# Modulation rows of a diffusion trunk: multiply-adds on VectorE and one sum over partitions in place of TensorE products

## The chip, the cores and the metric

The kernel runs on one core of a Trainium2 chip. A core has five engines with instruction queues of their own: TensorE (PE; its weight loads are listed apart as PEld), VectorE (DVE), ScalarE (ACT), GpSimd (POOL) and SyncE (SP), which here only issues DMAs. TensorE writes to PSUM, which has eight banks of 512 fp32 columns over 128 partitions; the other operands lie in SBUF. The metric is the device time of one execution in microseconds. The kernel before took 1547.54, 1547.64 and 1549.52 us in three runs, 1547.64 in the median.

## The reference

One inference step of two interleaved layers, in fp32, with width 1024, for 512 latent tokens and 128 context tokens. Layer 0 mixes by neighbourhood attention over a grid of 8 by 64 (NA), layer 1 by grouped-query attention with rotary positions (GQA). A gated feed-forward net with a convolution of width three (FFN) follows each. Around every sub-layer stand RMS norms, and a shift, a scale and a gate that come from a condition vector:

```python
def adaln(cond, w, b):
    m = jax.nn.silu(cond) @ w + b
    return jnp.split(m[..., None, :], 6, axis=-1)
...
    sh_ap, sc_ap, g_ap, sh_fp, sc_fp, g_fp = adaln(c_ctx, ada_w[l], ada_b[l])
    sh_as, sc_as, g_as, sh_fs, sc_fs, g_fs = adaln(c, ada_w[l], ada_b[l])
    hp = rmsnorm(xp, norm_mix_pre[l]) * (1.0 + sc_ap) + sh_ap
    ...
    xs = xs + g_as * rmsnorm(os_.reshape(bs, ts, -1) @ w_o, norm_mix_post[l])
    hs = rmsnorm(xs, norm_ffn_pre[l]) * (1.0 + sc_fs) + sh_fs
```

There are two condition vectors (latents, context), so one modulation row of a layer is a product of a 2x1024 matrix with 1024x1024 weights, plus a bias, times a norm's gain where there is one. Each layer has six such rows.

## The kernel before

The program runs through the stages input norm, NA, its output projection, FFN 0, GQA, its projection, FFN 1. Products with weights are made of three fp32r products of high and low parts: ScalarE rounds a weight tile to its high part `wh`, VectorE or GpSimd subtracts for the low part `wl` (`wsplit`, L174 to L180), TensorE multiplies.

The NA stage runs over 16 heads. For each head (class `Head`), TensorE forms the scores `s` of four slots, VectorE adds the bias table and finds the extremum in one operation on PSUM (L964), ScalarE takes the exponential `p` with its sum (L968), VectorE takes the reciprocal `rc` (L971), GpSimd scales `p` with it (L972), TensorE turns `p` into `tp` (L120), VectorE or ScalarE copies it out as `pk` (L985, L987), and TensorE multiplies with the values (`po`). GpSimd also builds the next head's bias table `tb` from a mask and shifted runs (L927, with two SBUF inputs) and the low parts `wl` (L180, the same). Into the steps of a head the program puts pieces of the projections to q, k and v, a `stream` of parts: one `fill` is one part, six products for q or k. VectorE helps to take q and k out of PSUM (`qs` at L878, `kl` at L850).

The order of TensorE's work is that of the program text: `mm` and `turn` chain each instruction to the one before. In the NA stage a written list per head sets it, `ORDER0`, `ORDER`, `ORDER2`: `f` is a fill, `s0` to `s3` the scores of the next head, `t0` to `t2` the turns of this one, `v` the values, `p0` to `p2` steps of the context, `a` a step of the modulation rows. The order on the other engines and of the DMAs is set by a scheduler with its own model of durations. Every queue is worked off in order: an instruction that waits holds those behind it.

Three modulation rows of layer 0 are made in the NA stage: index 2 (gate of the mixer, times a gain), 4 (scale of the FFN, with 1 added and times a gain) and 3 (shift of the FFN). Generator `ada_work` does it: each step loads two blocks of 128 features by 1024 columns (`wr<-in_ada_w`, L293) and makes eight products with two blocks that were loaded a step before. The stationary operand is 32 columns of `scolp`, of which the first two hold the two conditions' features; the moving operand is the raw block, in four pieces of 256 columns that go to four groups of 32 output partitions of one PSUM bank, `ada`. The bank collects over eight blocks. Then VectorE adds the bias (L319) and applies the gain (L322), and two small DMAs store the row to `modrow`, from where it is broadcast in the next stages (L352). The same generator makes the other rows later in the program.

## Time and profile before

| What | Value |
|---|---|
| median of three runs | 1547.64 us (1547.54 to 1549.52) |
| span of the profiled execution, first to last instruction | 1546.0 us |
| what the median has beyond that span | 1.64 us |
| granted TensorE clock, mean | 0.999 |
| TensorE busy in the span | 1512.8 us (98%) |
| VectorE busy in the span | 1024.1 us (66%) |
| ScalarE, GpSimd busy | 854.2 us (55%), 701.8 us (45%) |
| first and last product of the three rows | 82.0 and 269.8 us |

The profile is one execution, instruction by instruction. A group's row gives line, engine, operation, output and inputs by the program's tile names, their shapes and the count; then the busy time and the mean of one in ns; then the engine's idle time just before them and what ended it. A row of the order of time gives start, length, engine, line and operation, with idle time before it in brackets. A row by stretch gives start and end, length, and for PE, PEld, DVE, ACT and POOL the busy time with the count in brackets, then the clock, the DMA engines' share and GB/s. An fp32 product stands in the trace as two records. Lines named L180 and the like are lines of the kernel before.

### The profile page before, as it was taken

Reading aid. Unit: us, or ns where it says so; the run is one execution under the profiler, and the core shown is the slowest. Engines: PE = TensorE matmul, PEld = TensorE weight load, DVE = VectorE, ACT = ScalarE, POOL = GpSimd, SP = SyncE. Lnnn points to the kernel's source line nnn. Section 1 sums busy time; section 2 is a strip of 40 time slices with the busy share of each in tenths; the row PEclk is TensorE's granted clock in tenths of the full one; section 3 lists DMA queues with packets and bytes.
Section 4 is the critical chain, followed back from the end, with each engine's and each line's share of the span. In section 5 each row is a group of like instructions: output and inputs, shape, how many; then the busy total and the mean of one; then the engine's idle time right before and its main releaser. Section 6 shows DMA issues by size and latency. Waiting matters only on the chain.

```text
span 1546.0 us, 26097 instructions
## 1 busy us (share of the span) xinstructions
PE 1512.8 (98%) x9709; PEld 1344.4 (87%) x9709; DVE 1024.1 (66%) x1648; ACT 854.2 (55%) x1624; POOL 701.8 (45%) x606
## 2 busy tenths in 40 slices
PE   6999999999999999999999999999999999999998
PEld 5988998888999999978887878878899999988886
DVE  4553453659877666756757877773988887786554
ACT  5665564646655555654544447763666655554443
POOL 1554463432355455525444464532235666542433
PEclk9999999999999999999999999999999999999999
DMA  9745454253565665388574421015433334447664
GB/s 318 210 122 159 122 132 116 64 190 124 183 224 177 221 190 162 114 277 272 178 234 155 129 69 42 2 40 190 153 114 115 119 111 156 132 164 252 226 221 131
DMA packets 196666, 243.99 MB, mean 158 GB/s; under 512 B 11484, under 2 KB 153020, under 8 KB 196540
## 3 DMA queue, kind: packets, MB, share of 16 engines
q1 hardware_dynamic: 186704, 235.74, 47.7%
q10 hardware_dynamic: 9836, 6.59, 2.5%
q8 instruction: 76, 1.25, 0.3%
q14 instruction: 50, 0.41, 0.1%
HBM read 214.38 MB, written 26.34 MB: 156 GB/s over the span
## 4 chain that ended last, share of the span: by engine, by line
PE 66%; DVE 5%; ACT 2%; issue 2%; POOL 1%; DMA 1%; POOLq 0%; DVEq 0%; ACTq 0%
PE acc L117 19%; PE ux L117 18%; PE uz L117 8%; PE gp L117 5%; PE uy L117 4%; PE po L117 3%; PE y L117 3%; PE s L117 2%; PE tp L120 2%; PE ada L117 1%; DMA wr<-in_ffn_w_up 1%; DVE t L1281 1%; ACT gp L1692 1%; PE tr L120 0%; DVE xo L400 0%
## 5 line engine op out<-in xcount | busy, mean ns | idle before, releaser
L180 POOL TENSOR_TENSOR wl<-wr,wh 128x1024 fp32r<-128x1024 f32 x70 | 173.3, 2480 | 238.5 <-ACT wh L178 223.5
L1204 POOL TENSOR_TENSOR wl<-wr,wh 128x1024 fp32r<-128x1024 f32 x76 | 183.5, 2435 | 46.9 <-ACT wh L1203 43.3
L117 PE MATMUL ux<-B,wh 128*128 128x322 f32 x832 | 200.1, 311 | 0.9 <-ACT u L1258 0.9
L1281 DVE SCALAR_TENSOR_TENSOR t<-C,cw,t 128x644 f32<-128x644 f32 x176 | 156.3, 888 | 51.3 <-ACT t L1279 50.7
L117 PE MATMUL acc<-wh,alo 128*128 128x512 f32 x440 | 172.3, 392 | 0.3 <-DVE alo L1173 0.3
L178 ACT CAST wh<-wr 128x1024 fp32r<-128x1024 f32 x140 | 145.6, 1048 | 48.5 <-DMA wr<-in_ffn_w_down 37.4
L117 PE MATMUL acc<-wh,ahi 128*128 128x512 f32 x440 | 171.9, 391 | 0.0
L117 PE MATMUL acc<-wl,ahi 128*128 128x512 f32 x440 | 171.8, 391 | 0.0
L117 PE MATMUL uz<-B,wh 128*128 128x322 f32 x640 | 156.2, 312 | 0.9 <-ACT v L1258 0.9
L117 PEld LDWEIGHTS ux<-B,wh 128*128 128x128 f32 x832 | 143.6, 189 | 3.4 <-issue 1.2
L1173 DVE TENSOR_TENSOR alo<-ain,ahi 128x384 fp32r<-128x384 f32 (+1 forms) x88 | 84.0, 973 | 84.9 <-ACT ahi L1171 84.0
L117 PE MATMUL ux<-B,wl 128*128 128x322 f32 x416 | 129.5, 311 | 2.7 <-DVE wl L1204 2.7
L117 PE MATMUL qk<-hT,wh 128*128 128x384 f32 (+1 forms) x512 | 122.4, 315 | 0.0
L117 PEld LDWEIGHTS uz<-B,wh 128*128 128x128 f32 x640 | 110.9, 189 | 4.3 <-ACT v L1258 1.5
L1204 POOL TENSOR_TENSOR vl<-wr,vh 128x1024 fp32r<-128x1024 f32 x38 | 96.3, 2535 | 24.6 <-ACT vh L1203 24.3
L1203 ACT CAST wh<-wr 128x1024 fp32r<-128x1024 f32 x84 | 84.8, 1049 | 40.8 <-DVE wr L1227 40.5
L1279 ACT ACTIVATE t<-C,cw 128x644 f32<-128x644 f32 x88 | 78.6, 893 | 47.8 <-DVE C L1309 40.3
L180 DVE TENSOR_TENSOR wl<-wr,wh 128x1024 fp32r<-128x1024 f32 x70 | 91.3, 1315 | 20.1 <-ACT wh L178 19.5
L117 PE MATMUL uz<-B,wl 128*128 128x322 f32 x320 | 99.6, 311 | 0.3 <-POOL wl L1204 0.3
L117 PEld LDWEIGHTS acc<-wh,alo 128*128 128x128 f32 x440 | 82.5, 188 | 18.8 <-DVE alo L1173 1.1
L117 PEld LDWEIGHTS acc<-wl,ahi 128*128 128x128 f32 x440 | 82.6, 188 | 17.9
L117 PEld LDWEIGHTS acc<-wh,ahi 128*128 128x128 f32 x440 | 82.6, 188 | 17.8
(259 smaller groups left out, 3857.7 us busy)
## 6 DMA issues: line engine op xcount, KB each, us to landing
wr<-in_ffn_w_up SPq DMA_DIRECT2D x88, 512.0 KB
wr<-in_ffn_w_down SPq DMA_DIRECT2D x88, 512.0 KB
wr<-in_ada_w SPq DMA_DIRECT2D x72, 512.0 KB
act<-act SPq DMA_DIRECT2D x44, 321.0 KB
wr<-in_na_w_qkv SPq DMA_DIRECT2D x24, 512.0 KB
mod<-modrow SPq DMA_DIRECT2D x20, 512.0 KB
ain<-act SPq DMA_DIRECT2D x44, 192.0 KB
wf<-in_ada_w SPq DMA_DIRECT2D x16, 512.0 KB
```

The costliest lines, as they stand in the source:

```text
L117: pe(nc.tensor.matmul(*a, **k))
L120: pe(nc.tensor.transpose(*a, **k))
L178: i = nc.scalar.copy(hi, raw)
L180: j = (low or nc.vector).tensor_sub(lo, raw, f32(hi))
L1173: pin(nc.vector.tensor_sub(lo[:, 0 : c1 - c0], ain[:, 0 : c1 - c0], f32(hi[:, 0 : c1 - c0])))
L1203: nc.scalar.copy(hl[0], src)
L1204: low.tensor_sub(hl[1], src, f32(hl[0]))
L1279: nc.scalar.activation(t, taps(0), AF.Identity, bias=cw[:, 3, n : n + 1], scale=cw[:, 1, n : n + 1])
L1281: nc.vector.scalar_tensor_tensor(t, taps(d), cw[:, w, n : n + 1], t, op0=ALU.mult, op1=ALU.add)
L1692: nc.scalar.activation(self.pt[i].rearrange("p (a b) -> p a b", a=2), sv, AF.Exp, bias=nm, scale=-1.0, accum_out=su)
```

## The change

For the three rows of the NA stage a new generator, `ada_vec`, takes the place of `ada_work`. It goes by half rows of 512 columns. A block is 128 features by 512 columns. For each of the two conditions VectorE multiplies the block by the condition's column of `scolp` (one number for each partition) and adds it to `acc`, the first block by a plain multiplication, the other seven by a multiply-add. After eight blocks `acc` holds 128 partial sums for each column, and TensorE adds them over the partitions: eight products with a stationary operand `one`, whose column q is one and the rest zero, moving 128 columns of `acc` at a time. VectorE adds the bias and applies the gain, now on 128x128, in place in `abias`, and the row's half is stored. The generator is advanced at every third fill after the first 20, and not by steps `a` of the written lists; `lag` leaves one more advance between the last multiply-add and the sum. `ada_work` itself stays for the other rows.

```diff
--- before.py
+++ after.py
@@ -39,7 +39,6 @@
 QW = T + 64
 NPT = 6
 NPK = 6
-NAR = 2
 OW = {0: 0, 2: 1, 4: 2}
 OEARLY = 2
 TH = 322
@@ -47,10 +46,10 @@
 NC = 3
 QKH = (slice(0, 256), slice(256, T))
 CTX = 2
-ORDER0 = "f f f t0 s0 f s1 t1 f f t2 f a f f s2 s3 f f f f f".split()
+ORDER0 = "f f f t0 s0 f s1 t1 f f t2 f f f s2 s3 f f f f f".split()
 ORDER = (
-    "f f t0 s0 f s1 t1 f f t2 f a f f s2 s3 f f f f f f".split(),
-    "p0 f f t0 s0 f s1 t1 f t2 p1 f f f v a p2 s2 s3 f f f".split(),
+    "f f t0 s0 f s1 t1 f f t2 f f f s2 s3 f f f f f f".split(),
+    "p0 f f t0 s0 f s1 t1 f t2 p1 f f f v p2 s2 s3 f f f".split(),
 )
 ORDER2 = (
     "t0 s0 s1 f f f t1 f f t2 f s2 f s3 f f f f f f f".split(),
@@ -328,6 +327,69 @@
                 for _ in range(n if steps == 1 else i < n):
                     load()
                 yield
+
+    def ada_vec(p, todo, lag=1):
+
+
+
+        one = p.tile([P, 2, 32], F32, name="one")
+        nc.gpsimd.memset(one, 0.0)
+        for q in range(2):
+            nc.gpsimd.memset(one[:, q, q : q + 1], 1.0)
+        bias = p.tile([P, P], F32, name="abias")
+        gr = p.tile([P, P], F32, name="again")
+        nc.gpsimd.memset(bias, 0.0)
+        nc.gpsimd.memset(gr, 0.0)
+
+        def pieces(row, half):
+            return row[512 * half : 512 * half + 512].rearrange("(j c) -> j c", j=4)
+
+        units = deque((l, idx, half, k) for l, idx in todo for half in range(2) for k in range(KC))
+        raws = deque()
+
+        def load():
+            if units:
+                l, idx, half, k = units.popleft()
+                c0 = idx * D + 512 * half
+                raw = p.tile([P, 512], F32, tag="wr", name="wr", bufs=3)
+                nc.sync.dma_start(raw, A["ada_w"][l, k * P : k * P + P, c0 : c0 + 512])
+                raws.append((l, idx, half, k, raw))
+
+        for _ in range(3):
+            load()
+        yield
+        while raws:
+            l, idx, half, k, raw = raws.popleft()
+            if k == 0:
+                acc = p.tile([P, 2, 512], F32, tag="acc", name="acc")
+                for q in range(2):
+                    nc.sync.dma_start(bias[q::32, :], pieces(A["ada_b"][l, idx * D : idx * D + D], half))
+                    if idx in gain_of:
+                        nc.sync.dma_start(gr[q::32, :], pieces(A[gain_of[idx]][l], half))
+            for q in range(2):
+                col = scolp[:, 2 * k + q : 2 * k + q + 1]
+                if k == 0:
+                    nc.vector.tensor_scalar(acc[:, q], raw, col, None, op0=ALU.mult)
+                else:
+                    nc.vector.scalar_tensor_tensor(acc[:, q], raw, col, acc[:, q], op0=ALU.mult, op1=ALU.add)
+            load()
+            if k < KC - 1:
+                yield
+                continue
+            for _ in range(lag):
+                yield
+            ps = bk.get("ada")
+            for q in range(2):
+                for j in range(4):
+                    mm(ps[32 * j : 32 * j + 32, 0:P], one[:, q], acc[:, q, j * P : j * P + P], start=q == 0, stop=q == 1)
+            nc.vector.tensor_add(bias, ps[:, 0:P], bias)
+            bk.put(ps)
+            if idx in gain_of:
+                nc.vector.scalar_tensor_tensor(
+                    bias, bias, 1.0 if idx in (1, 4) else 0.0, gr, op0=ALU.add, op1=ALU.mult
+                )
+            for q in range(2):
+                nc.scalar.dma_start(pieces(modrow[l][idx][q], half), bias[q::32, :])
 
     def drain(gen):
         for _ in gen:
@@ -1051,13 +1113,15 @@
 
         work = stream()
         l_ada = ExitStack()
-        ada0 = ada_work(
-            l_ada.enter_context(pool("ada")), l_ada.enter_context(pool("adar", NAR)), NAR, 1, ((0, 2), (0, 4), (0, 3))
-        )
+        ada0 = ada_vec(l_ada.enter_context(pool("ada")), ((0, 2), (0, 4), (0, 3)))
+        fills = [0]
 
         def fill(n=1):
             for _ in range(n):
                 next(work, None)
+                fills[0] += 1
+                if fills[0] > PRO and fills[0] % 3 == 0:
+                    next(ada0, None)
 
         fill(PRO)
         next(ada0)
@@ -1074,8 +1138,6 @@
                 if step == "f":
                     if i < len(order) - 1 or h % 4 or not h:
                         fill()
-                elif step == "a":
-                    next(ada0, None)
                 elif step[0] == "s" and nxt:
                     nxt.scores(int(step[1]))
                 elif step[0] == "t":
```

Where the instructions now stand on VectorE, at two places of the NA stage. The first is where the q and k of the first pair of heads are taken out of PSUM, up to the first scores (`kl`, `kh`: low and high part of k; `s,nm`: scores with their extremum). Before:

```order
L850 TENSOR_TENSOR kl_620<-tk,kh_754 64x128
L849 CAST kh_754<-qk 64x256
L850 TENSOR_TENSOR kl_620<-qk,kh_754 64x256
L849 CAST kh_753<-qk 64x384
L850 TENSOR_TENSOR kl_619<-qk,kh_753 64x384
L849 CAST kh_754<-qk 64x384
L850 TENSOR_TENSOR kl_620<-qk,kh_754 64x384
L964 ISA s,nm<-s,tb_615 128x384
```

With the change (L911 and L912 are the former L849 and L850, L1026 the former L964):

```order
L912 TENSOR_TENSOR kl_619<-qk,kh_750 64x256
L374 SCALAR_TENSOR_TENSOR acc<-wr,scolp,acc 128x512
L911 CAST kh_751<-qk 64x256
L912 TENSOR_TENSOR kl_620<-qk,kh_751 64x256
L374 SCALAR_TENSOR_TENSOR acc<-wr,scolp,acc 128x512 x2
L911 CAST kh_750<-qk 64x384
L912 TENSOR_TENSOR kl_619<-qk,kh_750 64x384
L374 SCALAR_TENSOR_TENSOR acc<-wr,scolp,acc 128x512
L911 CAST kh_751<-qk 64x384
L912 TENSOR_TENSOR kl_620<-qk,kh_751 64x384
L1026 ISA s,nm<-s,tb_615 128x384
```

Four multiply-adds of the first half row now stand among these steps, ahead of the first scores. The second place is some 80 us later, where the scores of slots 2 and 3 of a head are reduced and their reciprocals taken (`rc`). Before:

```order
L850 TENSOR_TENSOR kl_622<-qk,kh_1830 64x256
L964 ISA s,nm<-s,tb_616 128x384
L964 ISA nm 128x1
L964 ISA s,nm<-s,tb_616 128x384
L964 ISA nm 128x1
L850 TENSOR_TENSOR kl_621<-qk,kh_1829 64x384
L971 RECIPROCAL rc<-su 128x1
L850 TENSOR_TENSOR kl_622<-qk,kh_1830 64x384
L971 RECIPROCAL rc<-su 128x1
```

With the change:

```order
L374 SCALAR_TENSOR_TENSOR acc<-wr,scolp,acc 128x512 x3
L1026 ISA s,nm<-s,tb_616 128x384
L1026 ISA nm 128x1
L1026 ISA s,nm<-s,tb_616 128x384
L1026 ISA nm 128x1
L912 TENSOR_TENSOR kl_621<-qk,kh_1887 64x384
L374 SCALAR_TENSOR_TENSOR acc<-wr,scolp,acc 128x512
L1033 RECIPROCAL rc<-su 128x1
L374 SCALAR_TENSOR_TENSOR acc<-wr,scolp,acc 128x512
L912 TENSOR_TENSOR kl_622<-qk,kh_1888 64x384
L1033 RECIPROCAL rc<-su 128x1
```

Three multiply-adds now stand ahead of the reductions, and one ahead of each reciprocal.

## The prediction

> **What bounds the kernel now.** First the page: spans, busy shares and the chain that ended last.
>
> ```profile
> span 1546.0 us, 26097 instructions
> PE 1512.8 (98%) x9709; PEld 1344.4 (87%) x9709; DVE 1024.1 (66%) x1648; ACT 854.2 (55%) x1624; POOL 701.8 (45%) x606
> PE 66%; DVE 5%; ACT 2%; issue 2%; POOL 1%; DMA 1%; POOLq 0%; DVEq 0%; ACTq 0%
> ```
>
> Then the busy time by stretch: the NA stage from where the new VectorE work starts to where it ends, and what follows up to the FFN.
>
> ```profile
> 52.00:272.00 220.00, 218.67 (x1695) 199.24 (x1694) 95.90 (x284) 127.70 (x344) 119.19 (x121) 1.00 0.53 141
> 272.00:335.00 63.00, 61.39 (x344) 50.57 (x343) 32.57 (x74) 37.07 (x94) 23.31 (x30) 1.00 0.30 94
> ```
>
> The columns behind the length are PE, PEld, DVE, ACT and POOL busy. TensorE is busy for 218.67 of 220 us at full clock, so the stage lasts as long as its products, and it can gain from idle time at most 1.3 us. VectorE has 124 us free, on average. A microsecond of products taken out is a microsecond won, as long as nothing that TensorE waits for comes later.
>
> **Products removed and added.** Groups of the stage, by form:
>
> ```profile
> L117 PE MATMUL ada<-wr,scolp 128*32 128x256 f32 x192 | 12.8, 385 | 0.0
> L117 PE MATMUL po<-ptp,vt 128*64 128x128 f32 x32 | 2.6, 282 | 0.0
> ```
>
> The 96 products of the three rows (each is two records) cost 12.8 us, 0.067 us a record. They go. Instead come six blocks of eight products with 128 columns, 96 records in all. No row has 32x128 products of this kind. If their price goes by columns, a record costs half of 0.067, and the six blocks 3.2 us; if by record, 6.4 us. The other 128-column group has 0.081 us a record with half as many column groups side by side, which halved is 0.04. I take 0.0375, 0.6 us a block and 3.6 us in all. **TensorE: 12.8 - 3.6 = 9.2 us less** (6.4 to 9.6).
>
> **VectorE work added.** 84 multiply-adds and 12 multiplications on 128x512, six additions and four gain steps on 128x128. Nearest rows (min/median/max ns in the first, mean of one in the second):
>
> ```profile
> L419 DVE SCALAR_TENSOR_TENSOR xm<-xm,ro,mod x30: 737/746/2883, 339.4 to 1110.5; 128x512 f32<-128x512 f32 x30
> L597 DVE TENSOR_SCALAR xT<-xT,gcol,hcol 128x512 f32<-128x512 f32 x8 | 4.3, 543 | 2.1 <-ACT hT L596 2.0
> ```
>
> The first is the same operation on the same shape, with both inputs in SBUF. So 14 x 0.75 + 2 x 0.54 = 11.6 us for each half row, with some 0.5 us for its addition and gain 12.1 us, six times. In all 73 us on top of 95.90: 169 of about 211 us. VectorE is not the bound on average. It is one in places, because the scheduler has put each half row's sixteen operations into one burst behind the sum of the half row before. These are the stretches of the bursts:
>
> ```profile
> 60.00:76.00 16.00, 15.79 (x107) 15.54 (x106) 10.81 (x32) 10.54 (x27) 9.64 (x9) 1.00 0.66 195
> 108.00:123.00 15.00, 15.00 (x128) 14.22 (x127) 5.37 (x16) 7.13 (x19) 7.23 (x9) 1.00 0.51 137
> 141.00:160.00 19.00, 19.00 (x144) 17.84 (x143) 10.16 (x30) 13.47 (x39) 10.21 (x10) 1.00 0.53 119
> 176.00:190.00 14.00, 14.00 (x124) 13.22 (x123) 5.38 (x16) 7.26 (x19) 7.20 (x8) 1.00 0.52 140
> 207.00:227.00 20.00, 20.00 (x148) 18.76 (x147) 10.21 (x31) 14.06 (x42) 10.98 (x12) 1.00 0.57 131
> 241.00:256.00 15.00, 15.00 (x129) 14.22 (x128) 5.38 (x16) 7.19 (x19) 7.22 (x9) 1.00 0.53 132
> ```
>
> VectorE's room is length minus busy: 5.2, 9.6, 8.8, 8.6, 9.8, 9.6 us. The first burst's ten multiply-adds of that stretch need 7.5 us, the others 12.1. So VectorE falls behind by 2.3, 2.5, 3.3, 3.5, 2.3 and 2.5 us by the ends of these stretches, if nothing else delays it.
>
> **Something else delays it.** Two places where VectorE and GpSimd both read two SBUF tensors:
>
> ```profile
> 756.76 5.21 POOL L180 TENSOR_TENSOR wl<-wr,wh 128x1024 fp32r<-128x1024 f32 x2
> 756.83 5.69 DVE L419 SCALAR_TENSOR_TENSOR xm<-xm,ro,mod 128x512 f32<-128x512 f32 x2 [1.08 <-POOL ro L379]
> ...
> 1187.33 2.90 POOL L1204 TENSOR_TENSOR vl<-wr,vh 128x1024 fp32r<-128x1024 f32 x1
> 1188.66 2.11 DVE L1224 TENSOR_TENSOR wr<-wr 128x512 f32<-128x512 f32 x1
> ...
> L1224 DVE TENSOR_TENSOR wr<-wr x40: 674/684/2125, 377.2 to 1365.2; 128x512 f32<-128x512 f32 x40
> ```
>
> Two multiply-adds of 0.75 us took 5.69 us while two GpSimd subtractions ran, and L1224, mostly 0.68 us, ended just after GpSimd's operation did (1190.77 against 1190.23). In this trace such an operation waits until the running one of GpSimd is over. In the stage GpSimd has much of that kind:
>
> ```profile
> L180 POOL TENSOR_TENSOR wl<-wr,wh 128x1024 fp32r<-128x1024 f32 x21 | 50.2, 2393 | 32.2 <-ACT wh L178 28.3 <-DMA tr<-in_k_rpb 3.8
> L927 POOL TENSOR_TENSOR tb<-mask,tr 128x256 f32<-128x256 f32 x44 | 37.9, 881 | 62.1 <-DVE nm L964 57.2 <-DMA tr<-in_k_rpb 4.6
> ```
>
> That is 88 of 220 us, 40%. VectorE's own operations here mostly read PSUM with one input and do not meet it; each new multiply-add does. One operation of GpSimd holds at most one of VectorE's; with one or two long and two short ones to a burst I take 1.3 us of waiting per burst, one long operation met in its middle and little more (bounds: none, and 4 us, two long ones met near their start).
>
> **Who waits for late VectorE.** Queued behind a multiply-add stand the score reductions, whose exponentials need their result, and the reciprocals, which GpSimd needs to scale the weights p that TensorE turns next. Around the third burst, then the fifth, the second, the fourth, the sixth, and last the first:
>
> ```profile
> 152.14 0.34 PE L117 MATMUL s<-kl,qs 128*128 128x384 f32 x1
> 152.84 0.56 DVE L964 CUSTOM_DVE_ANT_0 s<-s,tb 128x384 f32<-128x384 f32 x1
> 156.28 0.16 DVE L971 RECIPROCAL rc<-su 128x1 f32<-128x1 f32 x1
> 157.06 1.14 POOL L972 TENSOR_SCALAR p<-p,rc 128x384 f32<-128x384 f32 x2
> 159.37 0.60 PE L120 MATMUL tp<-ident,p 128*128 128x128 f32 x4
> ...
> 223.53 1.16 POOL L972 TENSOR_SCALAR p<-p,rc 128x384 f32<-128x384 f32 x2
> 225.89 0.60 PE L120 MATMUL tp<-ident,p 128*128 128x128 f32 x4
> ...
> 122.28 1.15 POOL L972 TENSOR_SCALAR p<-p,rc 128x384 f32<-128x384 f32 x2
> 127.36 0.60 PE L120 MATMUL tp<-ident,p 128*128 128x128 f32 x4
> ...
> 188.71 1.15 POOL L972 TENSOR_SCALAR p<-p,rc 128x384 f32<-128x384 f32 x2
> 193.79 0.60 PE L120 MATMUL tp<-ident,p 128*128 128x128 f32 x4
> ...
> 255.24 1.15 POOL L972 TENSOR_SCALAR p<-p,rc 128x384 f32<-128x384 f32 x2
> 260.32 0.60 PE L120 MATMUL tp<-ident,p 128*128 128x128 f32 x4
> ...
> 66.53 0.55 DVE L850 TENSOR_TENSOR kl<-qk,kh 64x384 fp32r<-64x384 f32 x1
> 67.94 0.34 PE L117 MATMUL s<-kh,qs 128*128 128x384 f32 x1
> 73.49 2.27 POOL L972 TENSOR_SCALAR p<-p,rc 128x384 f32<-128x384 f32 x4
> 75.82 0.33 PE L120 MATMUL tp<-ident,p 128*128 128x128 f32 x1 [0.21 <-POOL p L972]
> ```
>
> At the third burst p ends at 158.20 and its turn starts at 159.37: a margin of 1.2 us. At the fifth it is 225.89 - 224.69, again 1.2 us. At the second, fourth and sixth it is 3.9 us (127.36 - 123.43, and so on). At the first the scores wait for kl with 0.9 us of margin, and the turns already wait for p: none.
>
> **The sum.** Stall of a burst: what VectorE is behind, plus 1.3, less the margin. First 2.3 + 1.3 = 3.6 us; third 3.3 + 1.3 - 1.2 = 3.4; fifth 2.3 + 1.3 - 1.2 = 2.4; fourth 3.5 + 1.3 - 3.9 = 0.9; second and sixth none. **Stalls 10.3 us** (bounds: 2, where the bursts also use the free time around their stretches, and 26, with 4 us of waits at all six). 9.2 won and 10.3 lost is +1.1 on the span: 1547.1. The median of the runs shown, 1547.64, lies 1.6 above that span, so **1549 us**.
>
> Terms at nothing. The weight rows come in 48 loads of half the size instead of 24, the same bytes; DMA is at 0.53 in the stage, and the loads that they precede in SP's queue are issued three buffers ahead. The bias and gain loads of a half row, twelve and eight against six and four, now wait for the row's store and hold SP's queue for it; without that cover of three buffers, the loads behind would come 2 to 3 us late once per half row. A bank of PSUM is no longer held for a whole row, which only helps. In FFN 0 the scheduler exchanges convolution steps and block sums on VectorE and ScalarE; TensorE has 1.6 us of idle time from 272 to 335, and I give this a bound of 1.5 us to either side.
>
> **Rivals.** *The cover holds* (0.31). Multiply-adds run in the idle places that the order gives them, GpSimd's waits fall into time that VectorE had anyway, and only the first burst, with no margin, costs 3 us: 1547.6 - 9.2 + 3 = 1541. For it speaks 124 us of idle VectorE time; against it the six stretches, in none of which the room suffices. [...] With 3 us of waits the same sum is 5.3 + 5.1 + 4.1 + 2.6 + 1.6 + 1.6 = 20.3 us, and 1547.6 - 9.2 + 20.3 = 1559. It decides from about 2 us of waiting per burst on, where the stalls pass 13 us. [...]
>
> **How the numbers follow.** My forecast has 0.42, the cover 0.31, the bound 0.24, dear operations 0.03. A measurement of this kernel tells 0.2%, 3.1 us, from no change: 1544.5 to 1550.7 is the same. My forecast's own range is 1544 to 1553: 0.30 of its 0.42 lies in that band, 0.10 above and 0.02 below. Of the cover 0.29 lies below and 0.02 in the band, and the bound and the dear operations lie above. So faster 0.31, same 0.32, slower 0.37. The range 1540 to 1558 leaves out a lower part of the cover (0.07), the upper half of the bound (0.10) and the dear operations: 2 in 10.
>
> **What would show it.** L117's ada group at some 3.6 us; the multiply-adds' median at 0.75 us, with a mean near 0.85 to 1.0 and single ones over 2 us beside GpSimd's wl. In the waits of the stage, TensorE's tp behind GpSimd's p and its s behind VectorE's kl, together about 10 us, nearly all around 62 to 80, 160 and 226 us. It is wrong if these waits are under 4 us (the cover), if waits appear in the second, fourth and sixth bursts as well (the bound), or if the time moves behind 335 us.

## The result, and the profile after

| | before | with the change |
|---|---|---|
| median of five runs, us | 1547.64 (1547.16 to 1549.52) | 1559.95 (1559.12 to 1562.13) |
| ratio, 95% interval | | 1.0080 (1.0068 to 1.0091) |
| span of the profiled execution, us | 1546.0 | 1557.3 |
| granted TensorE clock, mean | 0.999 | 0.994 |

The change makes the kernel 12.3 us slower; 1549 was forecast, and 1558 was the upper end of the range. Names and lines below are those of each kernel's own listing: in the changed kernel L116 is `mm`, L119 `turn`, L179 `wl`, L374 the multiply-add, L372 the plain multiplication, L911 and L912 `kh` and `kl`, L940 `qs`, L1034 `p`, L1079 `ol`.

From the page of the changed kernel, span and busy times:

```profile
span 1557.3 us, 26100 instructions
PE 1511.6 (97%) x9613; PEld 1345.1 (86%) x9613; DVE 1106.2 (71%) x1749; ACT 850.2 (55%) x1624; POOL 716.4 (46%) x609
```

Its busy time by stretch (start and end, length, busy PE, PEld, DVE, ACT, POOL, then granted clock, DMA share, GB/s):

```profile
52.00:272.00 220.00, 207.39 (x1532) 192.36 (x1531) 173.09 (x378) 121.59 (x336) 132.28 (x116) 0.98 0.51 134
272.00:335.00 63.00, 59.82 (x353) 48.75 (x353) 30.83 (x77) 32.40 (x85) 17.47 (x24) 0.95 0.18 55
60.00:76.00 16.00, 11.77 (x65) 11.21 (x64) 14.17 (x30) 7.12 (x18) 6.12 (x4) 0.89 0.72 224
...
71.30:74.70 3.40, 3.38 (x11) 3.29 (x12) 2.81 (x6) 3.35 (x6) 1.78 (x1) 0.50 0.37 113
231.70:235.10 3.40, 3.40 (x15) 3.30 (x13) 2.88 (x6) 1.96 (x8) 1.26 (x2) 0.50 1.02 332
293.20:300.00 6.80, 5.84 (x16) 4.68 (x17) 4.69 (x11) 6.68 (x15) 4.35 (x4) 0.50 0.25 87
```

TensorE now idles 12.6 of the 220 us from 52 to 272, against 1.3 before, and 3.2 of the 63 us behind, against 1.6. New is the clock column: three stretches of 3.4, 3.4 and 6.8 us at half clock. Before, the clock is 1.00 in every stretch shown.

What TensorE waited for between 52 and 335 us, by the view of waits (us in total, times, longest), first with the change, then before:

```profile
PE s L116 <- DVE kh L911: 4.1, 1, 4.1
PE tp L119 <- POOL p L1034: 3.7, 7, 1.0
PE tk L119 <- ACT kp L954: 3.2, 1, 3.2
PE tp L119 <- DVE qs L940: 2.6, 4, 1.0
PE sp L116 <- DVE kl L912: 1.5, 1, 1.5
```

```profile
PE tp L120 <- DVE qs L878: 1.4, 2, 1.0
...
PE tp L120 <- POOL p L972: 0.7, 2, 0.5
PE tk L120 <- ACT kp L892: 0.2, 1, 0.2
```

The new operations of the changed kernel as groups, from 52 to 290 us (busy time in us, mean of one in ns, then the idle time ahead of them):

```profile
L374 DVE SCALAR_TENSOR_TENSOR acc<-wr,scolp,acc 128x512 f32<-128x512 f32 x84 | 78.3, 962 | 1.2 <-DMA wr<-in_ada_w 0.9
...
L116 PE MATMUL ada<-acc,one 128*32 128x128 f32 x96 | 3.9, 279 | 0.0
```

Shortest, median and longest of the multiply-adds in ns, by the view of that tile:

```profile
L374 DVE SCALAR_TENSOR_TENSOR acc<-wr,scolp,acc x84: 721/746/2881, 53.2 to 266.7; 128x512 f32<-128x512 f32 x84
```

**Where the time came from.** For TensorE's products that both programs have, I subtracted the start times of the two traces. With the change they start 1.5 us earlier at 52 and 66 us (of before's trace), 7.3 us later at 77, 6.1 at 272, 10.65 at 300 and 11.8 at 1540. The lead of 1.5 us arises before the first new instruction runs; in the profiles of this study the same place lies between 1.7 us ahead of before's and 0.4 us behind it, so I count it out. What is left is 13.2 us:

| Term | forecast | found | how found |
|---|---|---|---|
| products out, sums in | -9.2 | -8.9 | 12.8 less the 3.9 of the group above |
| first burst, 66 to 77 us | 3.6 | 8.8 | shift from -1.5 to 7.3 |
| the other bursts, 77 to 272 us | 6.7 | 7.7 | shift falls by 1.2, with 8.9 of products in it |
| 272 to 300 us | 0 | 4.5 | shift from 6.1 to 10.65 |
| behind 300 us | 0 | 1.1 | shift from 10.65 to 11.8 |

**The first burst.** The timeline of the changed kernel (start and length in us, engine, line, operation, count, and in brackets the wait ahead of it and what ended it):

```profile
51.06 6.37 POOL L989 TENSOR_TENSOR tb<-mask,tr 128x256 f32<-128x256 f32 x6
...
51.79 1.50 DVE L372 TENSOR_SCALAR acc<-wr,scolp 128x512 f32<-128x512 f32 x2 [2.10 <-DMA wr<-in_ada_w]
...
53.22 2.64 DVE L374 SCALAR_TENSOR_TENSOR acc<-wr,scolp,acc 128x512 f32<-128x512 f32 x2
...
56.65 4.14 DVE L374 SCALAR_TENSOR_TENSOR acc<-wr,scolp,acc 128x512 f32<-128x512 f32 x2 [0.34 <-DMA wr<-in_ada_w]
...
57.40 5.64 POOL L179 TENSOR_TENSOR wl<-wr,wh 128x1024 fp32r<-128x1024 f32 x2
...
70.13 0.55 DVE L911 CAST kh<-qk 64x384 fp32r<-64x384 f32 x1
...
70.74 0.45 PE L116 MATMUL s<-kh,qs 128*128 128x384 f32 x1 [4.10 <-DVE kh L911]
...
75.52 2.69 DVE L374 SCALAR_TENSOR_TENSOR acc<-wr,scolp,acc 128x512 f32<-128x512 f32 x1
...
78.69 0.16 DVE L1033 RECIPROCAL rc<-su 128x1 f32<-128x1 f32 x1
```

Two pairs of multiply-adds, 3.0 us of work, take 6.8 us beside GpSimd's tables and `wl`: the second pair ends at 60.79, and the two `wl` go on to 63.04. From there VectorE has no pause, `kh` ends at 70.68, and TensorE waits 4.1 us for it ahead of the scores. Behind the stall the clock is 0.50 for 3.4 us. At 75.52 another multiply-add takes 2.69 us beside a `wl`, 1.9 us more than its usual 0.75; the reciprocals stand behind it, p needs them, and the turns wait three times for p (0.5, 0.9 and 1.0 us). In the shift of the products the 8.8 us are 4.3 for the stall, 2.0 for the half clock and 2.5 for the turns.

**272 to 300 us.** The same view around `ol` and `kp`, first of the changed kernel, then of the one before:

```profile
286.65 2.40 POOL L179 TENSOR_TENSOR wl<-wr,wh 128x1024 fp32r<-128x1024 f32 x1
...
287.23 3.23 DVE L1079 TENSOR_TENSOR ol<-of,oh 128x640 fp32r<-128x640 f32 x2 [0.78 <-ACT oh L1078]
...
290.46 0.26 DVE L912 TENSOR_TENSOR kl<-tk,kh 64x128 fp32r<-64x128 f32 x1
...
294.16 0.48 PE L119 MATMUL tk<-ident,kp 128*128 128x128 f32 x1 [3.18 <-ACT kp L954]
...
294.29 0.77 PE L116 MATMUL y<-wh,oh 128*128 128x512 f32 x1
...
299.13 0.63 PE L116 MATMUL y<-wh,ol 128*128 128x512 f32 x1
```

```profile
275.40 0.82 DVE L1017 TENSOR_TENSOR ol<-of,oh 128x640 fp32r<-128x640 f32 x1 [2.13 <-ACT oh L1016]
...
285.44 0.33 PE L120 MATMUL tk<-ident,kp 128*128 128x128 f32 x1 [0.19 <-ACT kp L892]
...
285.52 0.48 PE L117 MATMUL y<-wh,oh 128*128 128x512 f32 x1
...
288.17 0.39 PE L117 MATMUL y<-wh,ol 128*128 128x512 f32 x1
```

The first two outputs are split into high and low parts in memory that the pool of the modulation rows gives free. The pool is closed behind the last row's sum. Before, the last row's addition ran at 270.2 us, the two subtractions `ol` at 275.4 and 276.8 us, and the `kl` that follow them from 282.5 us on. With the change the last row's addition runs at 282.4 us, and the `ol` stand right ahead of these `kl`. There they meet a `wl`, take 3.23 us instead of two times 0.82, `kl`, `kh` and `kp` come late in turn, and TensorE stalls for 3.18 us. Twelve products `y` then take 4.8 us from the first start to the last, where they took 2.65 before: half clock.

### The profile page after: what moved, and what is told of

It is laid out like the page before. It is cut to its first block, busy times and chain, and to the rows that moved or that the text cites. A ratio compares the mean times of both kernels' runs of the same rounds, so it can differ in the third digit from the quotient of the medians.

```text
span 1557.3 us, 26100 instructions
## 1 busy us (share of the span) xinstructions
PE 1511.6 (97%) x9613; PEld 1345.1 (86%) x9613; DVE 1106.2 (71%) x1749; ACT 850.2 (55%) x1624; POOL 716.4 (46%) x609
## 4 chain that ended last, share of the span: by engine, by line
PE 65%; DVE 5%; ACT 2%; issue 2%; POOL 1%; DMA 1%; POOLq 0%; DVEq 0%; ACTq 0%
PE acc L116 19%; PE ux L116 18%; PE uz L116 8%; PE gp L116 5%; PE uy L116 4%; PE po L116 2%; PE y L116 2%; PE s L116 2%; PE tp L119 2%; PE ada L116 1%; DMA wr<-in_ffn_w_up 1%; DVE t L1343 1%; ACT gp L1754 1%; PE tr L119 0%; DVE xo L462 0%
## 5 line engine op out<-in xcount | busy, mean ns | idle before, releaser
L179 POOL TENSOR_TENSOR wl<-wr,wh 128x1024 fp32r<-128x1024 f32 x70 | 175.4, 2510 | 239.3 <-ACT wh L177 239.1
L116 PE MATMUL ux<-B,wh 128*128 128x322 f32 x832 | 200.4, 312 | 0.9 <-ACT u L1320 0.9
L116 PE MATMUL acc<-wh,alo 128*128 128x512 f32 x440 | 172.4, 392 | 0.3 <-DVE alo L1235 0.3
L116 PE MATMUL acc<-wh,ahi 128*128 128x512 f32 x440 | 172.0, 391 | 0.0
L116 PE MATMUL acc<-wl,ahi 128*128 128x512 f32 x440 | 171.9, 391 | 0.0
L116 PE MATMUL uz<-B,wh 128*128 128x322 f32 x640 | 156.2, 312 | 1.4 <-ACT v L1320 1.4
L116 PEld LDWEIGHTS ux<-B,wh 128*128 128x128 f32 x832 | 143.7, 189 | 3.9 <-ACT u L1320 2.1
L116 PE MATMUL ux<-B,wl 128*128 128x322 f32 x416 | 129.6, 312 | 2.7 <-DVE wl L1266 2.7
L116 PE MATMUL qk<-hT,wh 128*128 128x384 f32 (+1 forms) x512 | 124.8, 319 | 0.0
L116 PEld LDWEIGHTS uz<-B,wh 128*128 128x128 f32 x640 | 111.0, 189 | 4.8 <-ACT v L1320 1.9
L179 DVE TENSOR_TENSOR wl<-wr,wh 128x1024 fp32r<-128x1024 f32 x70 | 91.3, 1315 | 17.8 <-ACT wh L177 17.2
L116 PE MATMUL uz<-B,wl 128*128 128x322 f32 x320 | 99.7, 311 | 0.3 <-POOL wl L1266 0.3
L116 PEld LDWEIGHTS acc<-wh,alo 128*128 128x128 f32 x440 | 82.6, 188 | 18.8 <-DVE alo L1235 1.1
L116 PEld LDWEIGHTS acc<-wl,ahi 128*128 128x128 f32 x440 | 82.6, 188 | 17.9
L116 PEld LDWEIGHTS acc<-wh,ahi 128*128 128x128 f32 x440 | 82.6, 188 | 17.7
```

The lines of the kernel that those rows point to most:

```text
L116: pe(nc.tensor.matmul(*a, **k))
L179: j = (low or nc.vector).tensor_sub(lo, raw, f32(hi))
```

## The experiments

Each run was timed on the same chip beside the kernel before (1547.6 to 1548.5 us there); ratios are to that. The theories: (A) VectorE is late behind its bursts and TensorE stalls; (C) what makes it late is the hold between VectorE's and GpSimd's operations; (D) VectorE has no room, so stalls only move; (E) the late splits are a cost of their own; (F) stalls halve the clock; (G) the work fits if it is spread out instead of done in bursts; (H) late weight blocks block VectorE's queue.

### VectorE's work left out

```diff
-                else:
-                    nc.vector.scalar_tensor_tensor(acc[:, q], raw, col, acc[:, q], op0=ALU.mult, op1=ALU.add)
-                if k == 0:
+                if k in (0, KC - 1):
```

> The 84 multiply-adds are left out: of each half row only the first and the last block are multiplied (plain multiplications, 24 in all of about 0.56 us), so the three rows come out without the other six blocks. Loads, sums over partitions, biases and stores stay. Theory A (VectorE is late behind its bursts, TensorE stalls, and the granted clock halves behind the longer stalls): all that the change lost goes with the multiply-adds, and the products' gain of 8.9 us is left: 1539 to 1541 us, idle TensorE under 3 us between 52 and 335 us, no half clock there. Rival B (the loss comes from the loads, the queue of the bias loads, or the sums): 1550 us or more, the stalls stay.

1545.58 us, ratio 0.9983 (0.9973 to 0.9992). The same with the late splits moved, as in the next section:

> The run without the multiply-adds (first and last block of a half row multiplied, the six between left out) and with the late splits: what the change would be if VectorE's work and the split cost nothing. Theory E (the split's 4.4 us add to the rest): 1545.6 less 4.4, 1541 us, with stalls of 2 to 3 us at 66 us left that come from waiting for weight blocks. Rival (the two effects overlap): 1544 us or more.

1544.23 us, ratio 0.9975 (0.9967 to 0.9984). So 14.4 us hang on the multiply-adds (1559.95 against 1545.58). But without them the two runs keep only 2.8 and 3.8 of the 8.9 us by which TensorE's work is less (the kernel before took 1548.41 and 1548.02 us beside them); the forecasts of 1539 to 1541 were too low, and theory A alone isn't enough. By the shift of the products, the first run still loses 3.8 us between 66 and 77 us (8.8 in the change), 0.3 from there to 272 (7.7 in the change) and 3.5 from 272 to 300 (4.5 in the change), where the stall for `kp` and the half clock stay. For the first of these losses the timeline of VectorE, here in the second run, shows the cause: VectorE waits for a weight block, with `kh` queued behind it.

```profile
68.06 0.88 DVE L372 TENSOR_SCALAR acc<-wr,scolp 128x512 f32<-128x512 f32 x2 [2.82 <-DMA wr<-in_ada_w]
68.97 0.55 DVE L909 CAST kh<-qk 64x384 fp32r<-64x384 f32 x1
```

The scores stall 2.2 us for that `kh`, and the shift grows by 3.7 us between 66 and 77 us. An operation that hardly costs anything held the queue because its block came late: 0.88 us of work behind a wait of 2.82. That is a second mechanism beside A, and I had put it at nothing.

### The late splits

```diff
                 osp0.extend([epool.tile(...) ...] for p in range(OEARLY))
-                for p in range(OEARLY):
-                    o_split(p)
...
                     head.turns(int(step[1]))
+                    if h == 12 and step == "t2":
+                        for p in range(OEARLY):
+                            o_split(p)
```

> The change with one thing moved: the splits of the first two outputs (oh on ScalarE, ol on VectorE) stand behind the third turn of head 12 in the text, not behind the last row's sum at the end of head 11. Theory E (the stall of 3.2 us at 291 us and the 6.8 us at half clock behind it come from the two subtractions ol that stand ahead of kl in VectorE's queue and meet wl): no stall over 1 us and no half clock between 275 and 305 us, 4 to 5 us less than the change: 1555 to 1556.5 us; up to 272 us the trace is the change's. Rival (kp is late for another reason, or the late split makes TensorE wait for oh and ol instead): 1559 us or more.

1557.32 us, ratio 1.0064 (1.0051 to 1.0076). TensorE's wait for kp in this run, and the stretch around it:

```profile
PE tk L119 <- ACT kp L954: 1.2, 1, 1.2
```

```profile
291.00:300.00 9.00, 7.58 (x41) 6.25 (x40) 8.68 (x17) 8.87 (x19) 3.40 (x4) 1.00 0.37 122
```

1.2 us remain of the 3.2, where 1 was expected at most, and the clock stays full. Between 272 and 300 us of before's trace the products' shift grows by 0.7 us, in the changed kernel by 4.5: 3.8 us gained at this place. The same edit takes this growth from 3.5 to 0.7 us without the multiply-adds (the two runs above), and from 3.7 to 1.0 us in a pair of runs further below. The medians of this run and the change differ by 2.6 us, and their intervals overlap in part. So theory E holds by the traces of three pairs of runs: more than a quarter of the 13.2 us found comes from the place of the splits, and most of it stays when there are no multiply-adds.

### One delay in the kernel before

Copies without use on VectorE, ahead of the first `kh`, eight and then four of them:

```diff
+                        if not p:
+                            for n in range(DELAY):
+                                oth = own_oth(n % 2)[1]
+                                z = kls[1][n % 2]
+                                i = nc.vector.tensor_copy(z[oth, :], f32(z[oth, :]))
+                                behind(i, qlast[0])
```

> The kernel before with one thing added: eight copies on 64x768 without use, some 4 us of VectorE, ahead of the first kh and kl, where the scores had 0.9 us of margin; nothing else moves. Theory F (TensorE's clock halves for the 3.4 us behind a stretch of 3.4 us of which it was idle for over about half): one stall of about 3 us and a half clock behind it; the scores' chain then makes up little: 3 to 6 us more than before, 1551 to 1554 us, of which 1 to 2 us are the clock. Rival G2 (VectorE has room enough behind this place to make all of it up, so a single delay costs less than its length): 1550 us or less.

> The same with four copies, some 2 us of VectorE. Theory F: a stall of about 1 us, no half clock behind it, 1 us more than before: 1548 to 1549.5 us; the difference to eight copies is more than the 2 us of work between them. Rival: half clock here too, 1550 us or more.

1557.74 us with eight, ratio 1.0064 (1.0050 to 1.0078); 1552.12 us with four, 1.0027 (1.0016 to 1.0038). VectorE's row with eight copies, what TensorE waited for, and the stretch behind the stall:

```profile
61.99 4.63 DVE L894 CAST kl<-kl 64x768 fp32r<-64x768 f32 x8
```

```profile
PE tp L121 <- POOL p L980: 4.2, 4, 2.3
PE s L118 <- DVE kh L851: 3.5, 1, 3.5
```

```profile
71.40:74.80 3.40, 3.40 (x13) 3.31 (x12) 2.98 (x8) 2.28 (x6) 2.35 (x1) 0.50 0.12 34
```

4.6 us of VectorE cost 9.7 us, 2.3 us cost 4.1: in the medians some twice the delay, more than I expected of either, and this where the scores had 0.9 us of margin. With eight copies the products' shift grows by 6.6 us up to 76 us (3.6 of stall, 1.9 of half clock behind it, 1.1 of turns that wait for p) and by 4.2 around 98 us, where p waits for a bias table that came late. GpSimd's order also moved by one `wl`, so these 4.2 us may be the order's and not the delay's. With four copies there is a stall of 0.6 us and no half clock, and the shift grows by 2.2 us up to 76 us and by 1.0 more up to 272. So by the traces these delays cost 1.4 times their length (6.6 us for 4.6 and 3.2 for 2.3, without the 4.2), and the room that VectorE has later gives nothing back.

### The hold

The multiply-adds replaced by plain multiplications of about the same length, with one SBUF input:

```diff
-                    nc.vector.scalar_tensor_tensor(acc[:, q], raw, col, acc[:, q], op0=ALU.mult, op1=ALU.add)
+                    nc.vector.tensor_scalar(acc[:, q], raw, col, None, op0=ALU.mult)
+                    nc.vector.tensor_scalar(acc[:, q, 0:176], raw[:, 0:176], col, None, op0=ALU.mult)
```

> Each multiply-add is replaced by two plain multiplications with one SBUF input, 512 and 176 columns, together about 0.75 us, the time of the multiply-add where nothing holds it; the sums over the blocks are left out. Same loads, same order of the work. Theory A in the form 'the amount of work and its place in bursts' : the stalls shrink only by the waits for GpSimd, about 1.3 us for each of three bursts: 1551 to 1557 us. Rival C (the two-input operations of VectorE and GpSimd hold each other, and without that the bursts fit): 1545 us or less, GpSimd's p back from 755 to about 600 ns in the mean and its wl from 2.5 to 2.4 us.

1567.83 us, 1.0135 (1.0115 to 1.0154): slower than the change, against both theories. The shorter multiplication's shortest, median and longest, by tile, and then two of them on VectorE's timeline:

```profile
L375 DVE TENSOR_SCALAR acc<-wr,scolp x84: 292/305/2523, 56.8 to 276.9; 128x176 f32<-128x176 f32 x84
```

```profile
56.80 4.82 DVE L375 TENSOR_SCALAR acc<-wr,scolp 128x176 f32<-128x176 f32 x2
```

Two operations of 0.3 us took 4.82 us, beside two `wl` of GpSimd from 56.55 to 61.51. The hold isn't a matter of two inputs on VectorE's side, and this run had twice as many operations to be held.

GpSimd's side changed, with the low parts of the weights left at zero:

```diff
+            for c in (slice(0, 820), slice(204, 1024)):
+                j = low.tensor_scalar(fl[:, c], fr[:, c], 0.0, 1.0, op0=ALU.mult, op1=ALU.mult)
-        j = (low or nc.vector).tensor_sub(lo, raw, f32(hi))
```

> GpSimd's subtractions for the low parts wl in the NA stage (two SBUF inputs, 2.4 us) are replaced by two operations with one SBUF input each, together about as long; the low parts are zero then, so the products with them add nothing. VectorE's work is the change's. Theory C: the five multiply-adds of over 2 us, which ran beside wl, take under 1.8 us (the bias tables still hold them), VectorE gets back about 9 us in five bursts, and of the stalls at 66 and 229 us most goes: 1549 to 1554 us. Theory A': 1557 us or more. If one-input operations of GpSimd hold the multiply-adds just as long, the long ones stay and the time does too.

1559.13 us, 1.0068 (1.0052 to 1.0085): no gain on the change, though the longest multiply-add is 1.4 us instead of 2.9. The multiply-adds by tile, and VectorE's timeline ahead of the first `kh`:

```profile
L380 DVE SCALAR_TENSOR_TENSOR acc<-wr,scolp,acc x84: 720/750/1391, 56.1 to 269.5; 128x512 f32<-128x512 f32 x84
```

```profile
66.25 0.75 DVE L380 SCALAR_TENSOR_TENSOR acc<-wr,scolp,acc 128x512 f32<-128x512 f32 x1 [3.37 <-DMA wr<-in_ada_w]
```

The edit took little of the holds away: all 84 multiply-adds take 75.7 us here, 78.3 in the change, and 60.8 in the next run, where nothing holds them. It also moved other work. GpSimd's tables start at 56.34 us instead of 51.06, SP issues the load of the fourth weight block at 63.35 us instead of 58.28, VectorE waits 3.4 us for that block, and the first stall is 7.5 us instead of 4.1. So the run doesn't tell what the holds cost.

The accumulator in two banks of PSUM, copied by ScalarE for the sum:

```diff
-                acc = p.tile([P, 2, 512], F32, tag="acc", name="acc")
+                acc = [bk.get("acc") for q in range(2)]
+                flat = p.tile([P, 2, 512], F32, tag="flat", name="flat")
...
+            for q in range(2):
+                nc.scalar.copy(flat[:, q], acc[q])
+                bk.put(acc[q])
```

> The accumulator of the multiply-adds lies in two banks of PSUM instead of SBUF; ScalarE copies it to SBUF before the sum over partitions (two copies of 128x512 per half row). So each multiply-add has one SBUF input. The rest is the change. Theory C (the hold between GpSimd's operations with two SBUF inputs and the multiply-adds makes VectorE late: in the change's trace 29 of the 96 operations took longer than 0.9 us, 18.7 us in all, and 3.9 us of that lie ahead of the first stall): the multiply-adds take about 0.75 us all, the stall of 4.1 us at 66 us goes under 1.5 us with the half clock behind it, the one at 229 us goes; the stall of 3.2 us at 291 us stays: 1549 to 1552 us. Theory A' (the amount of work in bursts, not the hold): stalls as in the change, 1556 us or more. A rival that comes with the edit: one bank fewer makes TensorE wait for banks.

1563.13 us, 1.0094 (1.0078 to 1.0111). The multiply-adds by tile, and the longest of TensorE's waits from 52 to 272 us:

```profile
L375 DVE SCALAR_TENSOR_TENSOR acc<-wr,scolp,acc x84: 724/749/756, 66.4 to 252.9; 128x512 f32<-128x512 f32 x84
```

```profile
PE tk L119 <- issue: 6.7, 4, 1.9
```

Here nothing holds the multiply-adds: 0.756 us is the longest. GpSimd's p takes 594 ns in the mean from 52 to 272 us, 755 in the change. The first burst costs 3.3 us instead of 8.8. But the work moved too: its first multiplication runs at 61.97 us (51.79 in the change), and one multiply-add stands ahead of the `kh` that the first scores need, where the change has nine. And there is one bank less, and TensorE now waits 6.7 us ahead of `tk` for nothing that the profile names, most likely the bank (not shown), and 8.3 us for VectorE's `kl` and `qs`, so that the run as a whole gains nothing. That the holds made the first burst dear is read from the change's own timeline (3.8 us lost ahead of a stall of 4.1); no run takes the holds away and leaves the rest in place, so what they cost the kernel in all isn't shown.

What in the chip makes the two engines hold each other isn't shown; the three runs show times alone, down to the plain multiplication of 0.3 us that took 2.5.

### Where the work stands

Started later (fill 47 instead of 20) and denser; then finished earlier and denser:

```diff
-                if fills[0] > PRO and fills[0] % 3 == 0:
+                if fills[0] > START and fills[0] % 9 in (0, 2, 4, 7):
```

> The new work starts behind fill 47 instead of fill 20 (second head instead of the scores of the first), and is advanced at four of nine fills instead of three of nine, to be done by the same head. Theory A: the first burst goes, and with it the stall of 4.1 us, the half clock behind it and the turns that waited (8.8 us of the shift between 66 and 77 us in the change's trace); the other stalls stay or grow a little by the denser work: 1551 to 1554 us, no idle TensorE over 0.5 us before 100 us. Rival D (VectorE has no room for the work anywhere, the stall only moves): 1558 us or more.

1570.48 us, 1.0143 (1.0128 to 1.0158). Rival D: TensorE stalls from 74 to 83 us, 6.3 us in four pieces, and later again.

```diff
+                if fills[0] > PRO and fills[0] % 12 in (0, 3, 5, 8, 10):
```

> The generator is advanced at five of twelve fills instead of four, so that its last sum is made about two heads before its pool is closed. In the change's trace the two subtractions ol stand behind that last sum and two score reductions, one takes 2.50 us beside GpSimd's wl where it took 0.82 before, and TensorE stalls 3.18 us at 291 us for kp, then runs 6.8 us at half clock. Theory E (this end costs 4 to 5 us, and it comes from where the last sum stands, not from the multiply-adds): no stall over 1 us between 275 and 300 us, no half clock there; the denser bursts cost up to 2 us more before: 1554 to 1558 us. Rival: the stall at kp has another cause and stays, 1560 us or more.

1577.61 us, 1.0191 (1.0176 to 1.0206). E's part came true (kp's stall is 0.45 us), but with a quarter more work per fill the products' shift grows by some 23 us more than in the change up to 272 us, where up to 2 were expected.

Each multiply-add kept behind the operation of VectorE that stands ahead of it in the text (`vlast` is set where `qs`, `kl`, `pk` and `rc` are made); then this and the moved splits together:

```diff
+                if not q and vlast[0]:
+                    behind(i, vlast[0])
```

> The change with one thing added: each multiplication and multiply-add is kept behind the operation of VectorE that stands before it in the text (a scheduling order, no wait), so the scheduler can't draw it forward into a burst behind the sum of the half row before; two at a time follow every third fill. Amount of work, loads and holds by GpSimd stay. Theory G (VectorE's burst is the bound of its stretch: in the change VectorE is busy for 7.62 of 8 us from 52 to 60 and for 16.2 of 18 us from 60 to 78): spread out, the work fits, the first stall goes under 1 us and the sum of the stalls between 52 and 272 us under 5 us; the stall at 291 us may stay: 1546 to 1552 us. Rival D (VectorE has no room, the stalls only move): 1557 us or more.

> Both edits, the late splits and the work kept to its place in the text. Theories E and G together: products 8.9 us less, stalls 2 to 5 us more than before, no half clock: 1542 to 1546 us. Rival D: 1553 us or more.

1575.48 us, 1.0181 (1.0164 to 1.0198), and 1576.31 us, 1.0178 (1.0164 to 1.0192). Theory G is wrong, the stalls only move, as in rival D. The first stall is gone as expected, from 66 to 72 us the shift grows by 0.4 us. But VectorE now waits for blocks, and TensorE for `qs` behind them (waits of the first run, 52 to 335 us):

```profile
DVE acc L376 <- DMA wr<-in_ada_w: 24.2, 17, 4.1
...
PE tp L119 <- DVE qs L944: 13.2, 6, 3.7
```

With the first block of all (3.7 us) this is 27.9 us; in the change, where the scheduler draws the multiply-adds to where its model has them ready, it is 3.0 us. Kept to a place, they meet blocks that are not there. The moved splits save 2.7 us between 272 and 300 us, and 3.4 us are lost ahead of that.

Two rows only, by hand in VectorE's long pauses, the third by products in the first two heads; and one row only, with the blocks loaded three ahead from ScalarE's queue. The written lists get steps `m` (one block) and `r` (the sum), here those of head 2:

```diff
-    "f f t0 s0 f s1 t1 f f t2 f f f s2 s3 f f f f f f"
+    "f f t0 s0 f s1 t1 f f t2 m m f f f s2 s3 m m m m f f f f f f"
```

> Two of the three rows go by multiply-adds, the third (the gate) by products as before, made in the first two heads; the 64 operations on VectorE do not start before the work that stands ahead of them in the text, and stand in the places where the trace of before shows VectorE idle for 2.6 to 6.5 us. Products cost 4.3 us, sums 2.6 us, in place of 12.8: 5.9 us less. Theory A: with the work in the gaps there is at most 2 us of new stall and no half clock: 1542 to 1544 us. Rival D (no room, because GpSimd and VectorE hold each other there too): 1547 us or more.

> Only the last row (shift of the FFN) goes by multiply-adds, 32 operations in heads 6 to 11, kept to places where the trace of before shows VectorE idle for over 2.5 us, their loads three blocks ahead from ScalarE's queue; the two other rows go by products in heads 0 to 5. Products 4.3 us less, sums 1.3 us more: 3.0 us less. Theory 'room' (where VectorE has room for the operation with its hold, nothing is lost): 1545 to 1547 us beside 1548 of before. Theory D (no room): 1550 us or more.

1556.57 us, 1.0056 (1.0041 to 1.0071), and 1556.28 us, 1.0051 (1.0039 to 1.0063). With two rows VectorE waits 17 us for blocks, and one such wait with a hold of 2.6 us makes TensorE stall 4.6 us at 148 us. With one row (and the splits moved) there is no stall over 1.0 us in the stage, though VectorE waits 11.5 us for blocks; but TensorE waits longer in FFN 0, and half clock follows (waits from 335 to 420 us, and the stretch):

```profile
PE ux L126 <- DVE wl L1290: 3.0, 1, 3.0
```

```profile
376.40:383.20 6.80, 6.17 (x23) 6.17 (x24) 5.29 (x7) 2.12 (x4) 0.00 (x0) 0.50 0.27 77
```

In before and in the change this wait is 1.4 us. VectorE's `wl` stands there behind a wait of 2.3 us for GpSimd (0.7 before); what makes GpSimd late isn't shown. Wait and half clock cost 4.1 us here, and the stage another 3.7. Even a third of the work, in the longest pauses, didn't pay, but with blocks that come late this isn't yet a test of the room alone.

### The loads' queue

Weight blocks from ScalarE's DMA queue, each one unit after its buffer came free; the bias loads at the fifth block. First with pinned multiply-adds and moved splits, then without the pinning, then with the accumulator in PSUM:

```diff
-                nc.sync.dma_start(raw, A["ada_w"][...])
+                nc.scalar.dma_start(raw, A["ada_w"][...])
```

> The run with both edits (late splits, multiply-adds kept to their place), and besides the weight blocks of the three rows are loaded from ScalarE's DMA queue instead of SP's, each one unit after its buffer came free; the bias and gain loads of a half row come at its fifth block, when the store before is long done. Theory H (in the pinned runs VectorE waited 27 us for weight blocks with TensorE's evictions queued behind it, because the loads stood in SP's queue behind loads that wait for buffers): these waits go under 5 us, the stalls of 2 to 4 us behind qs go, 1548 to 1556 us; what is left are the holds beside GpSimd, about 20 us of VectorE. Rival (the queue is not it, the loads are late by their own buffers): VectorE still waits over 15 us, 1565 us or more.

> The run with the late splits only (multiply-adds drawn forward into bursts as in the change), with the same new queue for the weight blocks. Theory A (in the bursts VectorE is the bound; loads are only 4 us of its waits there): the time stays near that of the run with the late splits, 1555 to 1558 us. Theory H for the bursts too: 1552 us or less.

> The run with the new queue, late splits and pinned multiply-adds, and the accumulator in two banks of PSUM. Multiply-adds take 0.75 us each, nothing holds them, GpSimd is back at 0.6 us for p; left are waits for banks, which cost the first run with PSUM some 8 us. Theory C+H (holds and late loads are all that VectorE lacked): 2 to 10 us less than the same run with the accumulator in SBUF. Rival (the bank that is missing costs more than the holds): more than that run.

1575.25 us, 1.0171 (1.0158 to 1.0184); 1560.50 us, 1.0082 (1.0068 to 1.0097); 1582.51 us, 1.0223 (1.0210 to 1.0237). VectorE's waits in the first:

```profile
DVE acc L381 <- DMA wr<-in_ada_w: 23.0, 16, 4.6
```

23.0 us, against 23.3 in the run with both edits that it starts from: the queue is not it, theory H is wrong in that form. Without the pinning the run starts from the one with the late splits and is no faster than that (1560.50 against 1557.32; 1552 or less was theory H's time). Beside the change, `kh` stalls the scores 2.0 us instead of 4.1, and waits for `qs` and p take it back (10.8 against 6.3 us). What is left, and was not tried, are the three buffers: before, a step's blocks were issued some 20 us ahead of their products (82.7 us, used at 102.5), while in the one-row run a block issued at 188.9 us was multiplied at 193.4, behind a wait of 2.4 us. With the accumulator in PSUM nothing holds VectorE, it waits 37 us for blocks, and banks are short as well.

### The clock

Products without use ahead of the scores that stall:

```diff
+        ps = bk.get("dummy")
+        for _ in range(24):
+            mm(ps[:, 0:P], ident, ident, start=True, stop=True)
+        bk.put(ps)
```

> 24 products of the identity with itself, 3.6 us of work for nothing, stand ahead of the first scores, where TensorE waits 4.1 us for VectorE's kh and kl in the change. Theory F (the granted clock halves behind a stretch in which TensorE was idle for more than about half of 3.4 us; that cost 2.1 us behind the first stall): no half clock between 60 and 90 us, the stall hides the dummies, and the time falls by about 2 us to 1557 to 1558.5 us. Rival (the half clock has nothing to do with the idle time): it stays, and the time is that of the change or up to 1 us more.

1564.40 us, 1.0107 (1.0092 to 1.0122).

```profile
66.00:78.00 12.00, 12.00 (x91) 11.97 (x90) 11.65 (x18) 4.89 (x10) 4.55 (x2) 1.00 0.65 191
78.00:92.00 14.00, 8.28 (x40) 7.01 (x39) 8.83 (x25) 6.19 (x18) 7.75 (x9) 0.77 0.44 114
```

With TensorE kept busy there is no half clock where there was one, so it came from the idle time. But VectorE isn't done any sooner (behind the first scores two multiply-adds take 2.8 and 2.3 us, where the change had one of 2.7), the stalls come from 78 us on instead, and the clock halves there. Filling TensorE's wait didn't help here, where the work that it waits for is the bound: 1564.40 us against 1559.95.

## Why the prediction failed, step by step

- **Products and sums**: right. 12.8 us went and 3.9 came (3.6 forecast, within 3.2 to 6.4); 8.9 gained.
- **The multiply-add's own time**: right, 746 ns in the median, as in the row of L419; that multiply-adds are dear of themselves, given 0.03, is shown by no run: the medians are 749 ns in the run with PSUM, 750 in the one with GpSimd's subtractions replaced and 752 with two rows.
- **"1.3 us of waiting per burst"**: the first step that failed. The 84 multiply-adds took 78.3 us, against 60.8 in the run where nothing holds them: 17.5 us of holds, 2.9 per burst, and beyond the 2 us from which I had called VectorE the bound. The first burst has the largest share: the two pairs up to 61 us lost 3.8 us, and one at 75.5 us another 1.9, together 5.7; the other bursts lost 1.7 to 2.9 us each. My bound of 4 us should have been the forecast there: already in the trace of before, tables and `wl` stand in GpSimd's queue without a pause from 52.6 to 62.4 us.
- **The first burst** (2.3 + 1.3 = 3.6): the term that was mis-sized most, it is 8.8 us. With 5.7 in place of 1.3, the same sum would have given 8.0. That the stall alone, 4.1, lies near 3.6 is luck: the 3.8 us of holds ahead of it leave little for the 2.3 us of missing room. The second step that failed is that a late VectorE costs its lateness once and at full clock. Behind the stall came 2.0 us for half clock, and 2.5 for turns that wait for p. In the kernel before, a delay of 4.6 us without any multiply-add cost 6.6 us up to 76 us.
- **The other bursts**: 6.7 forecast, 7.7 found. That is near partly by luck: the places are only in part the forecast ones (151.8, 165.0, 219.1 and 229.3 us), and half clock behind the last of them is in it. From the first operation to the last, the second to sixth bursts took 18 to 24 us, where I had reckoned with stretches of 14 to 20.
- **"Terms at nothing"**: the three-buffer cover was wrong in kind. I looked at what the loads hold up in SP's queue; what they hold up is VectorE's. In the change that wait is small (3 us), in the runs that keep the work to a place it is the largest.
- **272 to 335 us**: the third step that failed. I gave this 1.5 us for FFN 0 and put the splits behind the last row's sum at nothing. 4.5 us were lost, 3.8 of them by the place of the splits. Of a step that is moved, what waits for its memory moves too.
- **The clock**: no term. It is in the numbers above: 6.8 + 3.4 + 3.4 us at half clock.
- **Rivals**: "the cover holds" is out. The rival at 1559, VectorE as the bound of every burst, was given 0.24; its waits of 3 us agree with the 2.9 found, and so does the time, but the way doesn't: its stalls were 20.3 us in all six bursts, while 16.5 were found, with none over 0.3 us in the second, fourth and sixth, and the splits made up the rest.

The terms found give 13.2 us where those forecast gave 1.1. The 12.1 us between are 5.2 of the first burst, 4.5 of the splits, 1.0 of the other bursts, 0.3 of the products and 1.1 behind 300 us; less the 1.5 of the earlier start that is 10.6, and the medians lie 11 us above the forecast.

## What to carry to other kernels

Where TensorE is busy 98% of the time, moving work to an engine that is 34% free is worth what the free time is made of: here pauses of 1 to 6 us between operations for which TensorE waits. An operation put into such a queue must have its input there, must not run beside an operation of GpSimd that holds it (2.69 us instead of 0.75 beside a `wl`), and must not push the next operation back; a delay of 4.6 us at a place with 0.9 us of margin cost 9.7 us, one of 2.3 us 4.1. Before a step that ends a pool is moved, look up what is built in that pool's memory.

## What the runs showed of the hardware

**Half clock stood on a grid of 3.41 us.** In every profile of the study the granted clock changes only at multiples of 3.41 us from one another. In the changed kernel it fell to 0.50 at 71.27, 231.69 and 293.13 us, for 3.41, 3.41 and 6.83 us, and in the 3.41 us ahead TensorE was idle for 2.96, 1.53 and 2.15 us. I cut the time from 52 to 420 us of the 18 profiles with more than one such change into that grid: of the full-clock cells, all 39 with more than 1.91 us of idle TensorE were followed by a cell at half clock, and of the 85 with 1.0 to 1.91 us only 5 (1.53 to 1.84 us of idle time). So a stall of 1.5 us may cost nothing more or, by an estimate of half a cell, 1.7 us more, and where it falls has a part in it: the one of 1.53 us at 229 us lay in one cell and halved the clock in the changed kernel; its counterpart of 1.52 us in the run with the moved splits lay across a line of the grid (0.16 and 1.36 us) and didn't. What else decides between 1.5 and 1.9 us, where 20 of 25 cells kept the clock, isn't shown.

**The hold isn't only for two inputs in SBUF**, on either side: VectorE's plain multiplications of 0.3 us took 2.5 us beside `wl`, and in the run with GpSimd's subtractions replaced two multiply-adds took 2.58 us instead of 1.50 at 72.0 us beside GpSimd's multiplications of one input. With the accumulator in PSUM no multiply-add was held: 0.756 us was the longest of 84.
